# A hybrid decoder step: S5 of the prompt's second half moves beside the first two quarters' FFN

## The chip, the cores and the metric

The kernel runs on one core of one Trainium2 chip, in one launch. The metric is the device time of one execution in microseconds. The core has five engines that run their own instruction streams in order: TensorE (PE; PEld is its weight load), VectorE (DVE), ScalarE (ACT), GpSimd (POOL) and SyncE (SP), which here only issues DMA transfers. A wait of an instruction holds everything behind it on the same engine.

## The reference

One layer for a prompt of 2048 tokens and for 8 single-token samples; every weight product is in float32. What is computed, cut to what matters:

```python
n = rmsnorm(x, norm1_g)
proj = n @ w_in                      # 512 S5 inputs | 1536 qkv | 512 z | 4 beta | 4 a
y_s5  = s5_mixer(u_s5, ...)          # diagonal state space: complex scan over time, gelu, gate
y_gdn = gdn_mixer(qkv, z, beta, a)   # gated delta rule, 4 heads of 128, chunks; short conv; norm; gate
x = x + concat(y_s5, y_gdn) @ w_out
y = conv_ffn(rmsnorm(x, norm2_g))    # h = x @ w_up; conv of 3 taps over time; silu(gate)*up @ w_down
x = rmsnorm(x + y, normf_g)
```

Both mixers and the FFN's conv carry state along the prompt, so the quarters of the prompt are worked on in the order of time.

## The kernel before, in words

The prompt is cut in four quarters of 512 tokens, q0 to q3; the 8 samples ride behind q0. Activations stand transposed, channels on partitions. Every large product is made three times from splits of its operands in a high and a low part, `hi*hi`, `hi*lo`, `lo*hi` (`mm3`; `mm24` does it for the 8 channel tiles of the model, 24 matmuls for one tile of 128 outputs). Each 128x1024 piece of weights is loaded by SP into `wr` (2 buffers) and split into `whi` (a copy on ACT) and `wlo` (a subtraction on DVE); these come out of a ring of 8 buffers, `NW`.

The program has three stages.

- **Prologue.** For all four quarters in the order 3, 2, 1, 0: `x_load`, `norm_first` (transposes on PE, squares, row scales; x^T goes to DRAM) and `s5_in`, which multiplies with the S5 part of `w_in` and writes the inputs `up` to DRAM as `uD`. Beside them `s5_setup` computes the S5 matrices in eight steps, one per batch of 4 groups, and writes them to DRAM (`ED`, `FD`, `TD`). In that loop GpSimd's temporary `op`, the tile `Fi` and the tile `Tt` share one buffer, and so a step passes it on three times.
- **Mixers.** The string `MIXERS` is the order of emission: `b` and `h` are the two parts of one of eight S5 batches (`s5_batch`), each over all 256 chunks of 8 tokens; `F`, `I`, `B` are front, inverse and back of a delta net head. A batch loads its inputs `U` and matrices, multiplies, rotates, scans (one scan instruction per group and quarter, with `s5_turn` between quarters), rotates back and multiplies again, and ends with `s5_gelu`.
- **FFN.** The string `FFN` mixes `r`, the next piece of the generator `rest`, with the delta net stages of later quarters. `rest` first does the output gate of S5 (`s5_glu`) for q0 and q1, then for q2 and q3, then `ffn` for each quarter: the output projection in two halves of the tokens (`ffn_out`, the DVE addition L1144), norm 2 of the first half beside the second, a few tiles of the up projection early (`UPS`, first half of the tokens, which cover the second half's norm), and then eleven pieces of two channel tiles each (up projection, conv, gate, `ffn_down`). `N` makes the next quarter's normed input again from x^T in DRAM (`norm_again`).

The strings give the order of emission; a scheduler of the build then orders each engine's instructions from it, so the order on the engines is fixed before the kernel runs.

The normed input of a quarter lies in one buffer of the pool `n` (tag `nT`), so a new one waits for the last reader of the old one. PSUM tiles come in twos: `mm` for projections, `f` for many small things, `d` for the down projection, `s` for S5 (given back after the mixers).

Of the kernel before, what the change touches and what calls it, by code (L numbers as in the profile page):

```python
# [43 lines left out]
FFN = "IBNFrrIrFrrrrSrrBFrIIBrrrFIrBBrNFrIFrrrrBIrrFrrBIrrrrBFrrrrINBrFIrFrrBFIrrrrIrBrBrrrrrrrFrrrrrIBrrrGrrrrrrrrrrrrrrrrrrrr"  # L44
# columns of the constants
# [36 lines left out]
def rsqrt_(nc, a, y, t):  # L82
    """y = a^-1/2; one Newton step after exp/ln."""
# [9 lines left out]
def rsqrt_cols(c, ss, n, scale, tag, rows=128, tmp=None):  # L93
    """(ss*scale + eps)^-1/2 for ss [rows, n]"""
# [6 lines left out]
# ---------------------------------------------------------------- constants  # L101
def consts(c):
# [13 lines left out]
    # per-channel weights as columns  # L116
# [17 lines left out]
    # GDN  # L134
# [4 lines left out]
    # w_in columns for beta, a: [hi 8 | lo 8] per k tile  # L139
# [15 lines left out]
    # Xi[p, r, i] = (i == 4 (p % 8) + r): four rows of a 32 x 32 identity per partition  # L155
# [8 lines left out]
def sample_halos(c):  # L164
    """contribution of the samples' conv states to their conv outputs: [channel, sample]"""
# [69 lines left out]
    # row scales on all partitions  # L235
# [13 lines left out]
def norm_samples(c, pre):  # L249
    """normed x^T of the samples, [channel, (k tile, sample)]"""  # L250
# [41 lines left out]
def wsplit(c, src, eng=None):  # L292
    """[128, 1024] of weights as hi and lo"""
# [6 lines left out]
def wcols(c, w, col, q=None):  # L300
    """w[:, col:col+128] as hi and lo, [128, k, 128]"""
# [10 lines left out]
def proj(c, q, nT, w, col):  # L312
    """w[:, col:col+128]^T n, one PSUM tile per block of tokens"""
# [31 lines left out]
def s5_setup(c):  # L345
    """S5 matrices to DRAM: per batch of 4 groups T, F (input), E (output), tables."""
# [5 lines left out]
    c.ab1 = cp.tile([128, 2, 32], F32, name="ab1")   # re | signed im (-, +)  # L352
# [938 lines left out]
def kernel(tc, inp, outp):  # L1291
# [7 lines left out]
    with ExitStack() as es:  # L1299
# [154 lines left out]
```

## Time and profile before

| | |
|---|---|
| device time, median of 3 runs | 2872.86 us (2869.67 to 2876.55) |
| span of the profiled execution, first to last instruction | 2874.3 us |
| PE busy | 2715.0 us, 94% |
| weight loads busy | 2337.9 us, 81% |
| DVE busy | 2176.9 us, 76% |
| ACT busy | 1476.0 us, 51% |
| POOL busy | 609.6 us, 21% |

The profiled execution has no time of its own beside its span; the span lies within the three runs. A busy share is an average over the three stages, which differ; the ends of matmuls are modelled and neighbours overlap, so how fast PE works is read from the distance of starts.

### The profile page before, as it was taken

The page shows a single profiled execution, that of the slowest core. Times are in us where ns is not written, and L with a number is a line of the kernel's source. Part 1 is how long each engine was busy: PE and PEld are TensorE (multiplying, and loading weights), DVE is VectorE, ACT ScalarE, POOL GpSimd, SP SyncE. Part 2 cuts the span into 40 slices and gives each one's busy share as a digit, 9 for nine tenths or more (in the row PEclk, how much of TensorE's full clock was granted, in tenths as well). Part 3 has the DMA queues.
Part 4 walks back from the last instruction along what each step waited for, and adds up shares of the span by engine and source line. Part 5 has one row for each costly group of instructions (what it writes and reads, how often), then busy time and mean ns, then how long its engine had stood idle before and what let it go on. Part 6 is the DMA issues. An engine that isn't in the chain of part 4 may idle for free.

```text
span 2874.3 us, 45554 instructions
## 1 busy us (share of the span) xinstructions
PE 2715.0 (94%) x16103; PEld 2337.9 (81%) x16103; DVE 2176.9 (76%) x4964; ACT 1476.0 (51%) x3051; POOL 609.6 (21%) x970
## 2 busy tenths in 40 slices
PE   6998788899999999998899999999999998999998
PEld 4798676786888999998887888878888787888887
DVE  8949898856688787778588687887768667676666
ACT  4446565653665554455564554555545445444444
POOL 4325332100121122222221100113211112211112
PEclk9999887898999999999999999999999999999999
DMA  7644433453644232233533333245333334523332
GB/s 205 199 134 132 113 109 92 105 133 104 182 110 117 77 103 87 89 97 111 155 115 109 100 91 98 84 137 174 93 96 97 90 93 144 157 88 96 95 97 74
DMA packets 457657, 329.30 MB, mean 115 GB/s; under 512 B 74960, under 2 KB 412249, under 8 KB 457412
## 3 DMA queue, kind: packets, MB, share of 16 engines
q1 hardware_dynamic: 447091, 297.77, 35.8%
q0 software_dynamic: 10336, 28.61, 3.4%
q8 instruction: 127, 2.08, 0.3%
q14 instruction: 103, 0.84, 0.1%
HBM read 279.29 MB, written 47.29 MB: 114 GB/s over the span
## 4 chain that ended last, share of the span: by engine, by line
PE 66%; DVE 17%; DMA 8%; ACT 4%; issue 3%; POOL 0%; SPq 0%; DVEq 0%; POOLq 0%; ACTq 0%
PE psmm L287 15%; PE psmm L288 15%; PE psmm L289 15%; PE psd L287 5%; PE psd L288 5%; PE psd L289 5%; DVE wlo L72 3%; DVE t L823 1%; ACT whi L71 1%; DVE X L907 1%; DMA xr<-xTD 1%; DMA mr<-mixT 1%; DVE x L1097 1%; DVE hh L649 1%; DMA wr<-in_w_out_dram 1%
## 5 line engine op out<-in xcount | busy, mean ns | idle before, releaser
L287 PE MATMUL psmm<-nT,whi 128*128 128x512 f32 (+2 forms) x3232 | 1115.5, 347 | 45.2 <-ACT whi L71 9.6
L288 PE MATMUL psmm<-nT,whi 128*128 128x512 f32 (+2 forms) x3232 | 1110.3, 344 | 4.8 <-DVE nT L224 3.0
L289 PE MATMUL psmm<-nT,wlo 128*128 128x512 f32 (+2 forms) x3232 | 1107.2, 343 | 1.7 <-POOL wlo L72 1.0
L287 PEld LDWEIGHTS psmm<-nT,whi 128*128 128x128 f32 x3232 | 622.5, 193 | 120.3 <-ACT whi L71 11.7
L288 PEld LDWEIGHTS psmm<-nT,whi 128*128 128x128 f32 x3232 | 624.5, 193 | 73.1 <-DVE nT L224 4.5
L71 ACT ACTIVATE whi<-wr 128x1024 fp32r<-128x1024 f32 x404 | 427.2, 1059 | 496.3 <-PE psmm L288 309.9
L289 PEld LDWEIGHTS psmm<-nT,wlo 128*128 128x128 f32 x3232 | 623.0, 193 | 72.4 <-issue 1.9
L72 DVE TENSOR_TENSOR wlo<-wr,whi 128x1024 fp32r<-128x1024 f32 x388 | 482.3, 1246 | 193.2 <-ACT whi L71 187.4
L1097 DVE TENSOR_TENSOR x<-psd,x 128x512 f32<-128x512 f32 (+2 forms) x464 | 255.6, 558 | 127.3 <-PE psd L289 125.2
L287 PE MATMUL psd<-gt,whi 128*128 128x512 f32 (+2 forms) x928 | 323.6, 350 | 12.7 <-DVE x L1097 10.4
L288 PE MATMUL psd<-gt,whi 128*128 128x512 f32 (+2 forms) x928 | 316.5, 342 | 0.0
L289 PE MATMUL psd<-gt,wlo 128*128 128x512 f32 (+2 forms) x928 | 314.6, 340 | 0.0
L1254 DVE SCALAR_TENSOR_TENSOR t<-raw,cc,t 128x512 f32<-128x512 f32 x352 | 271.5, 772 | 37.1 <-ACT t L1251 27.5
L1255 POOL COPY halo<-raw 128x2 f32<-128x2 f32 x176 | 49.6, 282 | 850.7 <-DVE raw L1250 765.9
L1251 ACT ACTIVATE t<-raw,cc 128x512 f32<-128x512 f32 (+1 forms) x176 | 127.2, 723 | 170.0 <-DVE raw L1250 156.7
L287 PEld LDWEIGHTS psd<-gt,whi 128*128 128x128 f32 x928 | 175.0, 189 | 42.5 <-DVE x L1097 18.8
L72 POOL TENSOR_TENSOR gt<-s,gt 128x512 fp32r<-128x512 f32 (+1 forms) x88 | 134.7, 1531 | 350.4 <-ACT gt L71 341.6
L288 PEld LDWEIGHTS psd<-gt,whi 128*128 128x128 f32 x928 | 175.1, 189 | 20.6
L289 PEld LDWEIGHTS psd<-gt,wlo 128*128 128x128 f32 x928 | 174.9, 189 | 20.8
L1107 POOL TENSOR_TENSOR sq<-sq 128x256 f32<-128x256 f32 (+1 forms) x112 | 109.8, 981 | 219.1 <-ACT sq L1105 213.1
L906 DVE TENSOR_TENSOR tm<-X,N 128x124 f32<-128x124 f32 (+30 forms) x496 | 125.4, 253 | 26.7 <-DMA N<-nD 17.6
L907 DVE TENSOR_TENSOR X<-X,tm 128x124 f32<-128x124 f32 (+30 forms) x496 | 129.6, 261 | 8.4
(503 smaller groups left out, 3666.5 us busy)
## 6 DMA issues: line engine op xcount, KB each, us to landing
wr<-in_ffn_w_up_dram SPq DMA_DIRECT2D x176, 512.0 KB
wr<-in_ffn_w_down_dram SPq DMA_DIRECT2D x88, 512.0 KB
wr<-in_w_in_dram SPq DMA_DIRECT2D x64, 512.0 KB
wr<-in_w_out_dram SPq DMA_DIRECT2D x64, 512.0 KB
xTD<-xT SPq DMA_DIRECT2D x32, 256.0 KB
N<-nD SPq DMA_DIRECT2D x16, 512.0 KB
mr<-mixT SPq DMA_DIRECT2D x32, 256.0 KB
xr<-xTD SPq DMA_DIRECT2D x32, 256.0 KB
```

What stands on the lines that cost most here:

```text
L71: nc.scalar.activation(hi, raw, AF.Copy)
L72: (eng or nc.vector).tensor_tensor(lo, raw, f32(hi), op=OP.subtract)
L287: nc.tensor.matmul(out, lhsT=wh, rhs=xh, start=first, stop=False)
L288: nc.tensor.matmul(out, lhsT=wh, rhs=xl, start=False, stop=False)
L289: nc.tensor.matmul(out, lhsT=wl, rhs=xh, start=False, stop=last)
L906: nc.vector.tensor_tensor(m, X[:, :, j:j + 1].to_broadcast(sh), N[:, j:j + 1, j + 1:].to_broadcast(sh), op=OP.mult)
L907: nc.vector.tensor_tensor(X[:, :, j + 1:], X[:, :, j + 1:], m, op=OP.add)
L1097: nc.vector.tensor_tensor(x2[:, j, b0:b1], p, x2[:, j, b0:b1], op=OP.add)
L1107: c.nc.gpsimd.tensor_tensor(acc[0], acc[0], s, op=OP.add)
L1251: nc.scalar.activation(t[:, :n], raw[:, 2:2 + n], AF.Copy, scale=w[2])
L1254: nc.vector.scalar_tensor_tensor(t[:, :QT], raw[:, j:j + QT], w[j], t[:, :QT], op0=OP.mult, op1=OP.add)
L1255: nc.gpsimd.tensor_copy(c.halo[:, ch], raw[:, QT:QT + 2])
```

## The change

Prologue and mixers now handle only the first half of the prompt: `x_load`, `norm_first` and `s5_in` for q1 and q0, and eight S5 batches over 128 chunks (`HC`), which leave the state in `hst`. Two generators are new. `second` (letter `p` in the string) does load, norm and S5 inputs of q3 and q2 among the pieces of q0's FFN; it takes its four x tiles from the ring of weights and loads and splits the S5 part of `w_in` again for each of the two quarters. `third` (letter `t`) does the eight S5 batches of the second half, and then the gate of q2 and q3, among the pieces of q1's FFN; its matrices lie in the buffer `nT` (`s5_room`, two places), its PSUM tiles are `f`, and every batch loads its matrices from DRAM a second time. `norm_again` falls away for q2. The string `FFN` is new, and `UPS` has three tiles instead of four.

```diff
-NW, NWR, NV, NG, NM, UPB = 8, 2, 8, 4, 9, 1
+NW, NWR, NV, NG, NM, UPB = 8, 2, 8, 4, 10, 1
-UPS = (0, NCT, 1, NCT + 1)
+UPS = (0, NCT, 1)
-UNQ = (3, 2, 1)
+UNQ = (3, 1)
...
+FFN = ("IBNFrIrFSrBIrr"
+       "FrBIrFrBIrBrprprprprprprprprprprr"
+       "NFrIrFrBIrFrBIrFrtBIrtBrttrttrttrttrttrrr"
+       "NrFrIrFrBIrFrBIrFrBIrBrrrrGrrrr"
+       "rrrrrrrrrrrrrrrrr")
...
-def s5_batch(c, t, sp):
+def s5_batch(c, t, half, mk, samples):
...
-        nc.sync.dma_start(U[:, g], c.uD[t * 64 + g * 16:t * 64 + g * 16 + 16].rearrange("c s m -> s c m"))
+        nc.sync.dma_start(U[:, g], c.uD[t * 64 + g * 16:t * 64 + g * 16 + 16, :, m0:m0 + HC].rearrange("c s m -> s c m"))
...
-    for q in range(4):
+    if half:
+        nc.vector.tensor_copy(hh[:, :, 0, 0], c.hst[:, gs])
+    else:
+        nc.vector.memset(hh[:, :, 0, 0], 0.0)
+    for q in range(2):
...
             elif s == "N":
-                st.q, st.h, st.n = st.q + 1, 0, NT()
-                norm_again(c, st.q, st.n)
+                st.q, st.h = st.q + 1, 0
+                st.n = st.n2 if st.q == 2 else NT()
+                if st.q != 2:
+                    norm_again(c, st.q, st.n)
                 st.col = gdn_cols(c, st.q, st.n)
...
-            order = (3, 2, 1, 0)
-            xs = x_load(c, 3, pre)
+            xs = x_load(c, 1, pre)
...
-            for q0 in (0, 2):
-                yield from s5_glu(c, q0, nT)
+            yield from s5_glu(c, 0, nT)
...
+        def second():
+            xs = x_load(c, 3, None)
+            n = NT()
+            rs = norm_first(c, 3, n, xs)
+            yield
+            yield from s5_in(c, 3, n, None, None, rs)
+            xs = x_load(c, 2, None)
+            st.n2 = NT()
+            norm_first(c, 2, st.n2, xs)
+            yield
+            yield from s5_in(c, 2, st.n2, None, None, None)
+        def third():
+            maker = s5_room(c, np_)
+            bs = [s5_batch(c, t, 1, maker(t), False) for t in range(8)]
+            next(bs[0])
+            for t in range(8):
+                if t < 7:
+                    next(bs[t + 1])
+                next(bs[t], None)
+                yield
+            s5_final(c)
+            yield from s5_glu(c, 2, None, NT)
...
-            w, p = wcols(c, c.w_up, ch * 128), c.ps("mm" if len(ups) < 2 else "d")
+            w, p = wcols(c, c.w_up, ch * 128), c.ps("mm" if len(ups) < 1 else "d")
```

What that does to the order on the engines is seen at three places. On PE, the first S5 product of the mixers, ahead of the change; `Fm` and `U` are the matrix and the inputs of a batch, and the matmuls around it are the delta net's projections of q0.

```order
L287 MATMUL psmm<-nT,whi 128x264
L636 MATMUL pss<-U,Fm 128x256 x4
L288 MATMUL psmm<-nT,whi 128x264
L289 MATMUL psmm<-nT,wlo 128x264
L287 MATMUL psmm<-nT,whi 128x264
```

The same place on PE after the change:

```order
L289 MATMUL psmm<-nT,whi 128x256
L633 MATMUL pss<-U,Fm 128x128 x4
L290 MATMUL psmm<-nT,wlo 128x256
L288 MATMUL psmm<-nT,whi 128x256
L289 MATMUL psmm<-nT,whi 128x256
```

The product has half the columns. It stood 715 rows into PE's stream, and now stands 499 rows into it: the transposes and S5 inputs of two quarters are no longer ahead of it.

On DVE, q1's FFN, in a piece in the middle of the quarter, ahead of the change: `raw` and `t` are the conv of the up projection, `x_6015` takes the down projection's sums, and `De`, `LT`, `AT` belong to a delta net head.

```order
L1250 TENSOR_TENSOR raw<-psmm,rs_16639 128x256
L885 SCALAR_TENSOR_TENSOR LT<-psf,hc,De 128x128
L886 SCALAR_TENSOR_TENSOR AT<-psf,hc,De 128x128
L885 SCALAR_TENSOR_TENSOR LT<-psf,hc,De 128x128
L886 SCALAR_TENSOR_TENSOR AT<-psf,hc,De 128x128
L1254 SCALAR_TENSOR_TENSOR t<-raw,cc,t 128x512 x2
L1097 TENSOR_TENSOR x_6015<-psd,x_6015 128x512
```

Such a piece of q1's FFN on DVE after the change; `nT` is now the room of the S5 batch, `hw` the turn between quarters, `hst` the state that the next batch of the same groups starts from:

```order
L1129 TENSOR_TENSOR x_5295<-psd,x_5295 128x512
L639 TENSOR_TENSOR nT<-nT 128x8x64
L1296 TENSOR_TENSOR s<-s,t 128x512
L1129 TENSOR_TENSOR x_5295<-psd,x_5295 128x512
L649 SCALAR_TENSOR_TENSOR nT<-rho,nT 128x64 x4
L989 SCALAR_TENSOR_TENSOR rv<-psb,col,vt 128x128
L642 COPY nT<-hst 128x4
L601 TENSOR_TENSOR hw_17624<-nT 128x4
L601 TENSOR_TENSOR hw_17634<-nT 128x4
L586 SCALAR_TENSOR_TENSOR ga<-ga,psf 128x512
L600 TENSOR_TENSOR hw_17624<-hw_17624,nT 128x4
```

The scans, turns and gelu of an S5 batch stand between the additions of the down projection, in one in-order stream with them.

On DVE, the boundary from q0's FFN to q1's, ahead of the change: the additions of the output projection's second half (L1144), norm 2 (L195) and the splits of weights (L72).

```order
L1144 TENSOR_TENSOR x_6015<-psmm,xr 128x256
L833 TENSOR_TENSOR t<-s,t 128x512
L97 TENSOR_SCALAR rkq_a<-ssq,epscol 128x8
L195 SCALAR_TENSOR_TENSOR nrm<-x_6015,cc,rq 128x256
L72 TENSOR_TENSOR wlo<-wr,whi 128x1024
L1144 TENSOR_TENSOR x_6015<-psmm,xr 128x256
L195 SCALAR_TENSOR_TENSOR nrm<-x_6015,cc,rq 128x256
L72 TENSOR_TENSOR wlo<-wr,whi 128x1024
```

The same boundary on DVE after the change, where L1176 is that addition, L196 that norm and L938 and L939 the two instructions of a step of the delta net's inverse:

```order
L1176 TENSOR_TENSOR x_5295<-psmm,xr 128x256
L939 TENSOR_TENSOR X<-X,tm 128x4x25
L993 TENSOR_SCALAR vn<-psb,hc 128x128
L196 SCALAR_TENSOR_TENSOR nrm<-x_5295,cc,rq 128x256
L938 TENSOR_TENSOR tm<-X,N 128x4x24
L73 TENSOR_TENSOR wlo<-wr,whi 128x1024
L939 TENSOR_TENSOR X<-X,tm 128x4x24
L73 TENSOR_TENSOR nT_5296<-nrm,nT_5296 128x256
L1176 TENSOR_TENSOR x_5295<-psmm,xr 128x256
```

From the first addition of q1's output projection to the first `raw` of its up projection DVE had 118 rows, none of them of an inverse, and now has 311, of which 124 are the steps of two inverses.

## Rows read from the trace of the kernel before

**Rows 1.** The page: busy time of the engines over the span.

```profile
PE 2715.0 (94%) x16103; PEld 2337.9 (81%) x16103; DVE 2176.9 (76%) x4964; ACT 1476.0 (51%) x3051; POOL 609.6 (21%) x970
```

**Rows 2.** Busy time by stretches of the front: us, engines, granted PE clock, DMA.

```profile
0.00:749.00 749.00, 650.49 (x3851) 546.96 (x3852) 578.67 (x1762) 386.48 (x979) 197.59 (x242) 0.89 0.48 135
749.00:2874.30 2125.30, 2064.50 (x12254) 1790.96 (x12253) 1598.18 (x3202) 1089.52 (x2073) 412.00 (x728) 0.99 0.37 107
212.00:507.00 295.00, 245.41 (x1539) 212.42 (x1539) 258.78 (x734) 171.50 (x465) 103.26 (x116) 0.86 0.41 113
507.00:749.00 242.00, 226.90 (x1226) 181.94 (x1225) 164.61 (x495) 122.42 (x303) 22.99 (x37) 0.89 0.46 123
```

**Rows 3.** Busy time by stretches of the FFN stage, same columns.

```profile
839.00:1313.00 474.00, 470.87 (x3712) 449.39 (x3711) 374.16 (x886) 244.68 (x488) 108.03 (x211) 1.00 0.33 93
1471.00:1915.00 444.00, 441.10 (x2159) 354.08 (x2157) 356.53 (x772) 234.09 (x457) 58.41 (x125) 1.00 0.34 99
...
1312.70:1471.00 158.30, 141.82 (x1033) 130.29 (x1032) 112.19 (x253) 87.61 (x194) 37.43 (x49) 0.96 0.47 139
```

**Rows 4.** Timeline of PE in q1's FFN: start, us, instruction.

```profile
1839.68 0.39 PE L287 MATMUL psmm<-nT,whi 128*128 128x512 f32 x1
1839.91 0.39 PE L288 MATMUL psmm<-nT,whi 128*128 128x512 f32 x1
```

**Rows 5.** S5 inputs and first S5 product: count, durations, first to last start.

```profile
L550 DVE TENSOR_TENSOR up<-psmm,rsB x12: 1042/1090/1180, 42.4 to 146.9; 128x512 f32<-128x512 f32 x12
L548 ACT ACTIVATE up<-psmm x8: 366/384/385, 167.8 to 194.5; 128x256 f32<-128x256 f32 x8
...
L636 PE MATMUL pss<-U,Fm x64: 377/379/634, 212.2 to 463.5; 128*128 128x256 f32 x64
```

**Rows 6.** GpSimd's `op` in the setup, and waits between 26 and 170 us (total, times, longest).

```profile
L484 POOL TENSOR_TENSOR op<-CTim,PB x8: 1052/1063/1964, 63.0 to 160.4; 128x512 f32<-128x512 f32 x8
...
POOL op L484 <- DMA TD<-Tt: 37.4, 5, 9.4
```

**Rows 7.** GpSimd's timeline in the setup: its shortest link.

```profile
92.27 1.06 POOL L484 TENSOR_TENSOR op<-CTim,PB 128x512 f32<-128x512 f32 x1 [6.94 <-DMA TD<-Tt]
...
101.64 1.96 POOL L484 TENSOR_TENSOR op<-CTim,PB 128x512 f32<-128x512 f32 x1 [2.57 <-ACT nT L223]
```

**Rows 8.** DVE between 212 and 507 us: instructions on `hh`, then groups by line.

```profile
212.00:507.00 295.00, 22.28 (x64) 13.25 (x64) 87.20 (x223) 13.24 (x64) 18.11 (x8) 0.86 0.41 113
...
L593 DVE TENSOR_TENSOR yv<-pss,ga 128x512 f32<-128x512 f32 x14 | 9.5, 679 | 3.8 <-ACT ga L592 3.7
L589 DVE SCALAR_TENSOR_TENSOR ga<-ga,pss 128x512 f32<-128x512 f32 x14 | 9.5, 676 | 2.8 <-ACT ga L588 2.8
...
L603 DVE TENSOR_TENSOR hw<-hw,tab 128x4 f32<-128x4 f32 x32 | 6.1, 200 | 1.9 <-ACT hw L602 1.8
```

**Rows 9.** Timeline of PE: float32 products of S5, and smaller ones of a delta net head.

```profile
503.32 0.59 PE L668 MATMUL pss<-hw,Es 128*128 128x256 f32 x2
503.75 0.59 PE L665 MATMUL pss<-U,Tm 128*128 128x256 f32 x2
...
224.55 0.38 PE L954 MATMUL psb<-Sst,kq 128*128 128x128 f32 x2
224.78 0.39 PE L955 MATMUL psb<-Sst,kq 128*128 128x128 f32 x2
```

**Rows 10.** Groups by line: transposes of x, splits of weights, steps of the inverse.

```profile
L215 PE MATMUL psf<-ident,xt 128*128 128x128 f32 x128 | 23.6, 311 | 2.9 <-DVE nT L224 2.0 <-DVE nrm L195 0.7 <-DVE cc L132 0.2
...
L72 DVE TENSOR_TENSOR wlo<-wr,whi 128x1024 fp32r<-128x1024 f32 x388 | 482.3, 1246 | 193.2 <-ACT whi L71 187.4
L906 DVE TENSOR_TENSOR tm<-X,N 128x124 f32<-128x124 f32 (+30 forms) x496 | 125.4, 253 | 26.7 <-DMA N<-nD 17.6
L907 DVE TENSOR_TENSOR X<-X,tm 128x124 f32<-128x124 f32 (+30 forms) x496 | 129.6, 261 | 8.4
```

**Rows 11.** First and last addition of the output projection: durations, first to last start.

```profile
L1144 DVE TENSOR_TENSOR x<-psmm,xr x64: 405/423/433, 749.1 to 2490.4; 128x256 f32<-128x256 f32 x56, 128x264 f32<-128x264 f32 x8
```

More of the change, by code (lines that the diff above doesn't have):

```diff
@@ L199, in x_load @@
 def x_load(c, q, pre):
-    xs = [pre.tile([128, 1024], F32, name="xt", bufs=6) for _ in range(4)]
+    xs = [pre.tile([128, 1024], F32, name="xt", bufs=6) if pre else c.W("xt", F32) for _ in range(4)]
     for i, x in enumerate(xs):
-        (c.nc.sync if q == 3 else c.nc.gpsimd).dma_start(x, c.x_p[q * QT + i * 128:q * QT + (i + 1) * 128, :])
+        (c.nc.gpsimd if q == 0 else c.nc.sync).dma_start(x, c.x_p[q * QT + i * 128:q * QT + (i + 1) * 128, :])
     return xs
@@ L542, in s5_in @@
         rows = slice(t * 128, t * 128 + 128)
-        up = pre.tile([128, QT], F32, name="up", bufs=UPB).rearrange("p (s m) -> p s m", s=8)
-        for b0, b1, p in projw(c, q, nT, ws[t]):
+        up = (pre.tile([128, QT], F32, name="up", bufs=UPB) if pre else c.V("up")[:, :QT]).rearrange("p (s m) -> p s m", s=8)
+        for b0, b1, p in projw(c, q, nT, ws[t] if ws else wcols(c, c.w_in, t * 128)):
             e = min(b1, QT)
@@ L578, in s5_states, with s5_gelu @@
     c.ysm = sp.tile([16, 32, 8], F32, name="ysm")
-def s5_gelu(c, sp, out, y, rows=128):
+def s5_gelu(c, a, out, y):
     nc = c.nc
-    n = int(np.prod(y.shape[1:]))
-    a = sp.tile([128, 512], F32, name="ga", bufs=2)[:rows, :n]
-    if len(y.shape) == 3:
-        a = a.rearrange("p (a b) -> p a b", a=y.shape[1])
     nc.scalar.activation(a, y, AF.Square, scale=math.sqrt(0.044715))
@@ L613, in s5_batch @@
     lo, hi = slice(0, 64), slice(64, 128)
[L614 removed]
+    m0 = half * HC
+    U = mk("U").rearrange("p (g m) -> p g m", g=4)
     for g in range(4):
[L616 to L618 removed]
+        nc.sync.dma_start(U[:, g], c.uD[t * 64 + g * 16:t * 64 + g * 16 + 16, :, m0:m0 + HC].rearrange("c s m -> s c m"))
+    Fm, tab, Tm, Em, Es = (mk(n) for n in ("Fm", "tab", "Tm", "Em", "Es"))
     nc.sync.dma_start(Fm[:, :512], c.FD[t])
@@ L651, in s5_batch @@
     yield
[L653 to L654 removed]
+    s5_turn(c, hh[:, :, 1, 64], Ct, St, c.hst[:, gs])
+    hw = v65(mk("Xw"))[:, :, :, 0:64]
     H = hh[:, :, :, 0:64]
[L656 to L673 removed]
+    nc.gpsimd.tensor_tensor(hw, H, St[:, :, None, 0:64].to_broadcast(sh), op=OP.mult)
+    tt(H, H, Ct[:, :, None, 0:64].to_broadcast(sh), op=OP.mult)
+    yv = mk("yv")
+    p = c.ps(c.s5ps)
+    for g in range(4):
+        o = p[:, g * HC:(g + 1) * HC]
+        nc.tensor.matmul(o, lhsT=T[:, g], rhs=U[:, g], start=True, stop=False)
+        oq = o.rearrange("p (q m) -> p q m", q=2)
+        nc.tensor.matmul(oq, lhsT=E[:, g], rhs=H[:, g], start=False, stop=False)
+        nc.tensor.matmul(oq, lhsT=Es[:, g], rhs=hw[:, g], start=False, stop=True)
+    s5_gelu(c, mk("ga"), yv, p)
+    for g in range(4):
+        nc.gpsimd.dma_start(c.yD[t * 64 + g * 16:t * 64 + g * 16 + 16, :, m0:m0 + HC].rearrange("c j m -> j c m"), yv[:, g * HC:(g + 1) * HC])
+    if not samples:
+        return
+    p = c.ps(c.s5ps)
     for g in range(4):
@@ L683, in s5_batch, with s5_tiles, mk, s5_room @@
     nc.scalar.activation(c.ysm[:, gs], p[:16, 32:64].rearrange("p (g b) -> p g b", g=4), AF.Copy)
+def s5_tiles(c, sp):
+    kinds = dict(U=("U", 2), hh=("hh", 2), Xw=("Xw", 2), yv=("yv", 2), ga=("ga", 2))
+    def mk(n):
+        tag, bufs = kinds.get(n, ("mat", NM))
+        return sp.tile([128, 520], F32, name=n, tag=tag, bufs=bufs)[:, :520 if n in ("tab", "hh", "Xw") else 512]
+    return mk
+def s5_room(c, pool):
+    room = pool.tile([128, 16 * NQ], F32, name="nT")
+    sizes = dict(U=512, Fm=512, Tm=512, Em=512, Es=512, tab=520, hh=520, Xw=520)
+    state = {}
+    def maker(t):
+        def mk(n):
+            if n not in sizes:
+                return c.V(n)[:, :512]
+            at = (t % 2) * sum(sizes.values()) + sum(list(sizes.values())[:list(sizes).index(n)])
+            return room[:, at:at + sizes[n]]
+        return mk
+    return maker
 def s5_sample(c, sp):
@@ L1390 @@
         c.hst = c.cp.tile([128, 32], F32, name="hst")
+        c.s5ps = "s"
         with tc.tile_pool(name="s5", bufs=1, side="right") as sp:
             s5_states(c, sp)
-            bs = [s5_batch(c, t, sp) for t in range(8)]
+            mk = s5_tiles(c, sp)
+            bs = [s5_batch(c, t, 0, mk, True) for t in range(8)]
             hs = list(bs)
@@ L1404 @@
         ps_s.close()
+        c.s5ps = "f"
         c.wl = W2(nc)
@@ L1418, in rest @@
                 xrs, fin = yield from ffn(c, q, x2, nT, xrs, fin)
+        def second():
[20 more added lines that the diff above has]
+            yield from s5_glu(c, 2, None, NT)
         rs = rest()
+        se, th = second(), third()
         for s in FFN:
@@ L1422 @@
                 next(rs, None)
+            elif s == "p":
+                next(se, None)
+            elif s == "t":
+                next(th, None)
             else:
```

101 lines of the change are left out of this document (37 added, 64 removed).

## The prediction, made before the run

> **What bounds the kernel now.** I read the page's busy times first, then busy times by stretch, and last the timeline inside a stretch. The page gives PE 94% of the span and DVE 76% [rows 1], which suggests that PE is the bound throughout. The stretches say otherwise. Up to the first addition of the output projection, at 749.1 us [rows 11], PE is busy 650.5 of 749.0 us and DVE 578.7; behind it PE is busy 2064.5 of 2125.3 us [rows 2]. So nearly 100 of PE's 160 idle microseconds lie ahead of the FFN. In the middle of a quarter's FFN nothing is free on PE: 470.9 of 474.0 us and 441.1 of 444.0 [rows 3]. Since the ends of matmuls are modelled, I check this with starts: two 512-column matmuls of q1 stand 0.23 us apart and each is drawn 0.39 us long [rows 4], so the engine takes the next one in all the time. What is put into such a stretch lengthens it by its full work.
>
> The stage ahead of the FFN has three parts with different limits. (1) Until 212.2 us, when the first S5 product starts, the S5 inputs and the setup run; the last input's `up` starts at 194.5 us [rows 5]. The setup is a chain: GpSimd's `op`, `Fi` and `Tt` share a buffer, so a step's second `op` waits for the store of the last step's `Tt`; `op` starts from 63.0 to 160.4 us, seven steps of 13.9 us, and waits 37.4 us in that window for that store [rows 6]. (2) From 212 to 507 us DVE is busy 258.8 of 295.0 us, PE 245.4: the S5 batches and q0's delta net, where DVE is nearest to full [rows 2]. (3) From 507 to 749 us PE is busy 226.9 of 242.0 us [rows 2]: the output gate of four quarters, and projections.
>
> So the change takes work from a stage that is partly idle and puts it where PE has nothing to give. What it wins is idle time ahead of the FFN; what it costs is the moved matmuls at full price, and more DVE work at the boundaries between quarters.
>
> **The change part by part.** The sum goes against the profiled span of 2874.3 us, 1.4 over the median of 2872.86, which I take off at the end.
>
> (a) *Prologue.* The inputs of the first two of four quarters start at 42.4 us and the last at 194.5 us [rows 5]. That is about 40 us for a quarter, so the inputs of two are done near 115 us. Then the setup is last. With today's links it ends near 168 us (the last `op` at 160.4, then `Fi` and `Tt`), and a first product stands near 174: a saving of 38. Its shortest link, from 92.27 to 101.64 us, is 9.4 us [rows 7], where others wait for busy engines; eight such would end 31 us earlier, a saving of 69. Half of the work beside it is gone but the engines' queues still hold the delta net's first projections, so I take a value between, the first product at 162: **-50** (-38 to -69).
>
> (b) *S5 batches on half the columns.* DVE's instructions on `hh` take 87.2 us between 212 and 507, the three groups of gelu and turns 9.5, 9.5 and 6.1 [rows 8]: 112 us, of which half, 56, goes away. DVE is busy 259/295 there, so the stretch shortens by 56 x 295/259 = **-65**. If fixed costs of the smaller instructions keep a third of the saving, it is -46; if waits of GpSimd, ACT and transfers shrink along more than in proportion, -85.
>
> (c) *The gate of q2 and q3* leaves part (3): 192 matmuls of 512 columns at 0.232 us [rows 4] are 44.5 us, in a stretch that PE fills to 227/242: 44.5 x 242/227 = **-47**.
>
> (d) *What FFN gets on PE.* S5 inputs of two quarters: 2 x 4 tiles x 24 = 192 matmuls, 44.5 us. The gate, 44.5 us. S5's second half: 128 products of 128 columns; a float32 product of 256 columns starts every 0.43 us, and 128-column ones of a delta net head 0.23 us apart [rows 9], so 128 x 0.215 to 0.23 = 27.5 to 29.5, if they don't need the time of the large ones (55). Half of the 128 transposes of x, 23.6 us drawn [rows 10] with overlap: 8. Sum 125; I take **+124** (100 to 152).
>
> (e) *The rest on DVE, ACT and the queues.* The S5 part of `w_in` is split twice more: 8 subtractions of 1.246 us [rows 10] are 10 us on DVE, and as many copies on ACT; norm 1 of two quarters moves in, and the second making of q2's normed input falls away; SP gets the matrices of eight batches again and the weights, some 48 loads. In the middle of a quarter DVE is busy 374 of 474 and 357 of 444 us [rows 3], so this lies beside PE: **0**. Without that cover, where PE waits for a split, up to +15.
>
> (f) *DVE at the boundary from q0 to q1.* It took 158.3 us with PE busy 141.8 and DVE 112.2 [rows 3]. Between the output projection's additions and q1's up projection DVE now has the 124 steps of two inverses, which average 0.257 us [rows 10]: 32 us, and other rows of heads, which brings DVE's work there to some 171 us by the counts of rows and their durations, and PE's to about 139. A boundary that took PE plus 16 idle could take DVE's 171 plus some idle: about 180 us, **+20**. Below, 0, if the steps fall into the gaps between additions; above, +59, worked out among the rivals (R1).
>
> (g) *One tile less in `UPS`.* Norm 2 of a second half has 24 matmuls of 256 columns less to hide it. At half of 0.232 us each they are 2.8 us; for three boundaries, where PE also waits somewhat longer, **+5** (0 to +17). Behind those norms stand the splits of weights on DVE [rows 10], which are late next.
>
> Sum: -50 -65 -47 +124 +0 +20 +5 = -13; 2874.3 - 13 = 2861; with the median's 1.4 less it would be 2860, and since I rounded moved work down in (d), I write **2862**.
>
> *A rule against the reading of a full PE.* The trace shows q2's middle stretch with PE busy 441 of 444 us, and the weight loads 354 [rows 3]. The Trainium skill ("Perfetto Trace Analysis", section "Identifying the Most-Contended Engine") holds matmul busy time to be a bad measure, because matmuls are pipelined, and wants the weight loads' busy share instead. By the share of the loads a fifth of that stretch would be free, and (d) would cost 100 instead of 124. By the starts, 0.23 us apart without a gap [rows 4], it costs 124, which stands in the sum.
>
> **The rivals.**
>
> R1, *the boundary q0 to q1 becomes DVE's* (slower). The inverses are chains of small steps in one in-order stream with the additions that free PSUM for the output projection, so PE stops for each; a step also waits for the delta net's matmuls, which stand behind the output projection on PE. For it: DVE's work at the boundary exceeds PE's for the first time, by my count 171 against 139. Against it: the steps are 0.25 us each, and the inverse's waits in the trace are small against its work [rows 10]. Then DVE keeps its idle time of today's boundary, 158.3 - 112.2 = 46 us, beside 171 of work: 217 us, +59 and not +20, and the sum is 2862 + 39 = 2901. It decides from 12 us beyond (f) for no gain, some 17 for a measurable loss.
>
> R2, *nothing is won*: the smaller S5 instructions keep their fixed cost, (b) comes out at -46 or so and part (2) is set by q0's delta net instead. -50 -46 -47 +124 +20 +5 = +6, less the 1.4: 2879; with 5 more from (a), 2874. In (b), that DVE is full to 88% only speaks for it.
>
> R3, *weight loads are the bound* (faster). The moved matmuls cost 100: 2838. The starts in [rows 4] speak against it; for it, that PE stands only at 81% by loads [rows 1].
>
> R4, *the setup doesn't get shorter*, and the first S5 product is held to 174 us or later by the chain and by the tables behind it: (a) is -30, and the sum 2882. [...]
>
> **How the numbers follow.** What a measurement of this kernel can tell from no change is about 0.2%, 5.7 us: 2867.1 to 2878.6. Chances: the forecast 0.38 and R3 0.12, both faster; R2 0.12, the same; R1 0.28 and R4 0.10, slower. That makes faster 0.50, same 0.12, slower 0.38. The forecast's own range, from the bounds of (b), (d) and (f) that move against each other, is 2840 to 2867. The range for all goes down to 2800 (the lower bounds of (a) and (b) together, -39, with 2838) and up to 2925 (2901 with the upper bounds of (e) and (g), +27).
>
> **What would show it.** Right: the first S5 product near 162 us (143 to 174); the first addition of the output projection near 749 - 162 = 587 us; behind it some 2274 us instead of 2125, PE full in the middle of each quarter and the stretches of q0 and q1 longer by the moved work (65 and 75); the boundary q0 to q1 near 180 us. Wrong: a first addition later than 610 us puts the fault in (a) to (c); if the stage behind is longer than 2290 us, PE idle for additions at the boundary shows R1, and PE idle in the middle of q1 shows waits of the second half's S5 batches, whose scans and gelu stand between the additions of the down projection on DVE; I hold these covered, since the batches are begun one ahead, and this would make the prediction wrong in a place where no row of before can tell.

## The result, and the profile after

The changed kernel took 2989.77 us, the median of 4 runs (2984.88 to 2996.21), beside 2871.7 us for the kernel before in the same session: a ratio of 1.0404 (95% interval 1.0384 to 1.0424). It is 118 us slower, where a gain of 11 us was forecast, and lies beyond the range's upper end of 2925. The profiled execution has a span of 2994.4 us.

The page's row of busy times, after, answers to [rows 1].

```profile
PE 2764.4 (92%) x16287; PEld 2378.4 (79%) x16287; DVE 2176.9 (73%) x4984; ACT 1482.4 (50%) x3055; POOL 622.1 (21%) x1010
```

DVE does what it did before, to the tenth of a microsecond, and PE is drawn 49 us busier; nothing on this row explains 120 us. The marks of the prediction come next: the S5 products of either half, and the additions of the output projection (count; shortest, median and longest in ns; first to last start in us).

```profile
L633 PE MATMUL pss<-U,Fm x64: 270/275/377, 170.5 to 342.3; 128*128 128x128 f32 x64
L633 PE MATMUL psf<-nT x64: 270/275/377, 1537.4 to 1694.9; 128*128 128x128 f32 x64
...
L1176 DVE TENSOR_TENSOR x<-psmm,xr x64: 408/422/433, 643.6 to 2608.2; 128x256 f32<-128x256 f32 x56, 128x264 f32<-128x264 f32 x8
```

The first product stands at 170.5 us (forecast 162, from 143 to 174). The first addition stands at 643.6 us, where 587 was forecast and 749.1 was the time before [rows 11]. So the stage ahead of the FFN won 105.5 us and not 162, and the FFN stage took 2350.8 us and not 2274. Busy times by stretch, after (stretch; its length; busy time of PE, weight loads, DVE, ACT and POOL with their counts; granted PE clock; DMA share; GB/s):

```profile
0.00:170.50 170.50, 131.47 (x817) 116.56 (x818) 137.76 (x495) 62.71 (x142) 67.18 (x79) 0.87 0.56 160
170.50:363.60 193.10, 173.96 (x1340) 163.08 (x1339) 155.19 (x440) 112.21 (x309) 81.09 (x111) 0.88 0.47 127
363.60:643.60 280.00, 239.19 (x1236) 187.38 (x1236) 188.69 (x629) 127.36 (x344) 23.35 (x43) 0.79 0.37 100
...
750.20:1192.90 442.70, 428.09 (x3312) 413.28 (x3311) 288.91 (x517) 203.89 (x353) 97.52 (x193) 0.97 0.36 107
1192.90:1439.20 246.30, 207.98 (x1319) 179.56 (x1317) 171.66 (x430) 127.02 (x291) 41.94 (x61) 0.90 0.39 112
1439.20:1895.80 456.60, 454.37 (x2245) 372.34 (x2244) 357.43 (x742) 247.39 (x464) 98.54 (x163) 1.00 0.43 123
1895.80:2093.60 197.80, 164.34 (x1035) 142.54 (x1034) 138.53 (x313) 101.91 (x224) 36.06 (x51) 0.92 0.44 127
```

Four rows stand out against [rows 2, 3]. The S5 stretch (second row) is 102 us shorter, but the stretch behind it, up to the output projection (third row), is 38 us *longer*, with the lowest granted clock of all, 0.79, although half of the gate's matmuls left it. The boundary q0 to q1 (fifth row; from the last `raw` of one quarter to the first of the next) grew from 158.3 to 246.3 us and the boundary q1 to q2 (last row) from 111.4 to 197.8; in neither is DVE full, 70% in both. q1's pieces (sixth row) are full, as forecast. The boundary q1 to q2 before, in the same columns:

```profile
1914.90:2026.30 111.40, 104.14 (x794) 99.10 (x793) 86.20 (x183) 62.52 (x135) 34.26 (x39) 0.97 0.54 162
```

To see what is work and what is loss, I count each PE record at the distance between starts that its shape has when PE runs through: 0.230 us for 512 columns, 0.117 for 256, 0.216 and 0.111 for a float32 record of 256 and 128 (the lower quartile of all distances in both traces). A stretch's length less this sum, both in us, is called PE's lost time here: pauses, and matmuls that start further apart. It is an estimate; another price for the small records moves single rows by up to 4 us, in both kernels alike.

| stretch | time before, after | work before, after | lost before, after |
|---|---|---|---|
| to the first S5 product | 212.2, 170.5 | 157.6, 102.7 | 54.6, 67.8 |
| to the last S5 product (first half) | 294.8, 193.1 | 190.0, 133.9 | 104.8, 59.2 |
| to the first output projection | 242.1, 280.0 | 191.3, 176.8 | 50.8, 103.1 |
| q0's projection and norm | 89.8, 106.6 | 77.0, 85.9 | 12.8, 20.7 |
| q0's pieces | 473.8, 442.7 | 454.9, 409.2 | 18.9, 33.4 |
| boundary q0 to q1 | 158.2, 246.3 | 126.9, 181.1 | 31.4, 65.2 |
| q1's pieces | 443.9, 456.6 | 427.6, 443.6 | 16.3, 13.0 |
| boundary q1 to q2 | 111.5, 197.8 | 95.8, 146.7 | 15.6, 51.1 |
| q2's pieces | 366.0, 418.3 | 360.8, 403.2 | 5.3, 15.1 |
| the rest | 482.0, 482.5 | 440.1, 439.5 | 41.9, 43.1 |
| sum | 2874.3, 2994.4 | 2522.0, 2522.7 | 352.3, 471.7 |

The work is the same, as it must be where the same products are only moved. All of the 120 us is lost time: 20 us more ahead of the FFN, where less was to be lost, and 99 more in it, 69 of them at two boundaries. The lengths hold one more thing: the boundaries hold 54 and 51 us more of PE's work, mostly of heads that stood in the pieces before. What such a loss looks like, on PE's timeline at the boundary q1 to q2, after (start, us, instruction, and the idle time before it with its releaser):

```profile
1933.16 0.66 PE L1228 MATMUL psd<-ident,x 128*128 128x128 f32 x4 [0.26 <-ACT yout L1230]
1942.70 0.61 PE L799 MATMUL psmm<-nT,wab 128*16 128x512 f32 x1 [8.89 <-ACT nT L72]
1943.11 0.41 PE L288 MATMUL psmm<-nT,whi 128*128 128x256 f32 x1
1943.32 0.42 PE L289 MATMUL psmm<-nT,whi 128*128 128x256 f32 x1
```

PE meets, in its order, the first product of the delta net's columns, whose input `norm_again` (letter `N`) is still to make, and pauses for 8.9 us. Behind the pause the 256-column matmuls of the output projection start 0.21 us apart instead of 0.117: the granted clock is at the lower of its two levels, 1.2 GHz. So the pause costs more than its length. PE's largest waits at the two boundaries (total us, times, longest), q0 to q1 first:

```profile
PE psmm L288 <- DVE x L1176: 6.7, 1, 6.7
PE psf L805 <- ACT abT L801: 6.7, 1, 6.7
...
PE psmm L288 <- DVE x L1176: 8.9, 3, 8.0
PE psmm L799 <- ACT nT L72: 8.9, 1, 8.9
```

Followed back on the other engines, three of these four longest waits (6.7, 6.7, 8.0 and 8.9 us) end in a transfer from or to DRAM that an engine meets in its order. Behind the 8.9 us for `nT` stands the load of x^T for `norm_again`. Behind the 6.7 us for the addition stands the load of an inverse's matrix (the tile `N`, not the letter): DVE waits for it, does 12 instructions of the inverse, and only then comes to the addition that PE waits for. Behind the 6.7 us for `abT` ACT waits 6.8 us for the store of a state. The lines of the addition's wait and of the load of x^T, in the order of time:

```profile
1296.66 0.88 DVE L938 TENSOR_TENSOR tm<-X,N 128x124 f32<-128x124 f32 x1 [6.09 <-DMA N<-nD]
1301.38 0.42 DVE L1176 TENSOR_TENSOR x<-psmm,xr 128x256 f32<-128x256 f32 x1
1301.86 0.58 PE L288 MATMUL psmm<-nT,whi 128*128 128x256 f32 x1 [6.74 <-DVE x L1176]
...
1941.23 0.75 DVE L196 SCALAR_TENSOR_TENSOR nrm<-xT,cc,rsB 128x512 f32<-128x512 f32 x1 [8.43 <-DMA xT<-xTD]
```

These four are 30 of the 72 us that PE pauses at the two boundaries; the rest is many short pauses.

What is there at the boundaries that was not? Counted by their lines, 2 fronts and 2 inverses of heads in the first (before: 1 and 0.1), 2 fronts and 1 inverse in the second (before: none of either). The new `FFN` string puts `N` and the next quarter's heads there, since the S5 work takes the buffer `nT` in the middle of the quarter.

### The profile page after: what moved, and what is told of

Its sections match the earlier page's. It is cut to its first block, busy times and chain, and to the rows that moved or that the text cites. A ratio compares the mean times of both kernels' runs of the same rounds, so it can differ in the third digit from the quotient of the medians.

```text
span 2994.4 us, 46166 instructions
## 1 busy us (share of the span) xinstructions
PE 2764.4 (92%) x16287; PEld 2378.4 (79%) x16287; DVE 2176.9 (73%) x4984; ACT 1482.4 (50%) x3055; POOL 622.1 (21%) x1010
## 5 line engine op out<-in xcount | busy, mean ns | idle before, releaser
L288 PE MATMUL psmm<-nT,whi 128*128 128x512 f32 (+2 forms) x3208 | 1114.5, 348 | 50.5 <-DVE x L1176 22.4
L288 PEld LDWEIGHTS psmm<-nT,whi 128*128 128x128 f32 x3208 | 622.0, 194 | 127.6 <-ACT t L852 15.6
L72 ACT ACTIVATE whi<-wr 128x1024 fp32r<-128x1024 f32 x412 | 435.1, 1059 | 549.5 <-PE psmm L289 358.7
L938 DVE TENSOR_TENSOR tm<-X,N 128x124 f32<-128x124 f32 (+30 forms) x496 | 119.5, 241 | 37.9 <-DMA N<-nD 24.6
L939 DVE TENSOR_TENSOR X<-X,tm 128x124 f32<-128x124 f32 (+30 forms) x496 | 126.1, 254 | 8.9
```

What stands on the lines that cost most here:

```text
L288: nc.tensor.matmul(out, lhsT=wh, rhs=xh, start=first, stop=False)
L938: nc.vector.tensor_tensor(m, X[:, :, j:j + 1].to_broadcast(sh), N[:, j:j + 1, j + 1:].to_broadcast(sh), op=OP.mult)
L939: nc.vector.tensor_tensor(X[:, :, j + 1:], X[:, :, j + 1:], m, op=OP.add)
```

## The experiments

Two theories stood at the start. T1: PE loses time where a head's chain stands beside too few independent matmuls, at the boundaries above all. T2: the moved S5 work itself costs more than its matmuls. Medians are set beside the kernel before in the same session, 2870.9 to 2873.5 us; ratios are to it, with their 95% interval.

**The heads spread.** In all strings below, only what differs from the changed kernel is shown, from q0's pieces to the end of q3's heads.

```diff
-prprprprprprprprprprrNFrIrFrBIrFrBIrFrtBIrtBrttrttrttrttrttrrrNrFrIrFrBIrFrBIrFrBIrB
+prpprpprpprpprpNrFrIFrBIrFrBIrrrrrrFBIrBrttrttrttrttrttrttrNFrIFrBIrrrrrrFrBIrFrBIrB
```

> The changed kernel with another order string only: the delta net heads of q2 and q3, which stood at the boundaries q0 to q1 and q1 to q2, begin in the last pieces of the quarter ahead, and the S5 batches of the second half run later in q1. Same work. Theory T1 (PE loses time where a head's chain stands beside too few independent matmuls, so at the boundaries): the two boundaries, 246 and 198 us, come back to about 180 and 115, some 15 to 30 us of it are given back in the pieces that take the heads, and the time falls by 50 to 120 us, to 2870 to 2940. Rival T2 (the moved S5 work itself costs more than its matmuls, by waits in the pieces where it stands): the time stays within 15 us of 2990.

2950.54 us (ratio 1.0268, 1.0242 to 1.0293): 39 us back. The two boundaries in its profile:

```profile
1287.00:1418.50 131.50, 111.31 (x863) 104.59 (x862) 97.65 (x243) 62.74 (x126) 36.90 (x43) 0.95 0.45 135
1943.10:2062.40 119.30, 106.06 (x821) 98.99 (x820) 95.41 (x233) 61.93 (x129) 29.89 (x39) 0.96 0.51 153
```

Lost time is 34 and 25 us there, against 65 and 51; q1's pieces lose 30 instead of 13. T2 falls as the cause of the boundaries: the S5 work stood in the same quarters. Of the 118 us, 77 remain.

**Three tiles in `UPS`, in the kernel before.**

```diff
-UPS = (0, NCT, 1, NCT + 1)
+UPS = (0, NCT, 1)
```

> The kernel before with three tiles in UPS instead of four, the first in the mm buffers and two in the d buffers, as after the change. T1 and T2 alike: three boundaries lose the cover of 24 matmuls of 256 columns, 2.8 us each or somewhat more: 2872 to 2890. If it were the cause of the slow boundaries, it would be 2950 and more.

2878.78 us (1.0018, 1.0003 to 1.0034): 5 us, which is term (g).

**The same with the heads at the boundaries.** S5, norm and gate of the kernel before, `UPS` of three, and its string from q0's projection on as the changed kernel's without its `p` and `t`. (With four tiles in `UPS` this order deadlocks, so the run above is its measure.)

```diff
-FFN = "IBNFrrIrFrrrrSrrBFrIIBrrrFIrBBrNFrIFrrrrBIrrFrrBIrrrrBFrrrrINBrFIrFrrBFIrrrrIrBrBrrrrrrrFrrrrrIBrrrGrrrrrrrrrrrrrrrrrrrr"
+FFN = "IBNFrrIrFrrrSrrBIrFrBIrFrBIrBrrrrrrrrrrrrNFrIrFrBIrFrBIrFrBIrBrrrrrrrrNrFrIrFrBIrFrBIrFrBIrBrrrrGrrrrrrrrrrrrrrrrrrr"
```

> The kernel before with three tiles in UPS (which alone measured 2878.8) and with the heads of q2 and q3 at the boundaries in the changed kernel's order; S5, norm and gate stand as before the change. T1 (a head's chain beside too few independent matmuls loses PE's time): after one string changed the boundaries q0 to q1 and q1 to q2 are 40 to 90 us longer, part of it the heads' own matmuls, and the time is 2915 to 2970. T2 (the moved S5 work costs more than its matmuls): 2865 to 2890.

2955.49 us (1.0284, 1.0266 to 1.0302): 77 us more than with `UPS` alone. The boundaries are nearly those of the changed kernel, 246.30 and 197.80 us there:

```profile
1222.30:1482.50 260.20, 208.30 (x1322) 178.54 (x1321) 181.93 (x448) 132.39 (x299) 43.94 (x61) 0.90 0.40 116
1861.60:2057.00 195.40, 164.35 (x1035) 142.72 (x1034) 138.54 (x313) 102.03 (x224) 38.11 (x51) 0.92 0.45 128
```

The order of the heads alone makes them, without any S5 work moved. The run also parts the 118 us: 5 for `UPS`, 77 for the order, and the 34 us from here to the changed kernel for the move itself. By lost time, the move costs 25 us in q0's pieces (8 here, 33 in the changed kernel, with the same heads there) and about 17 ahead of the FFN.

**Norm and S5 inputs into the gate's stretch, all heads spread.** Besides the string, `second` keeps row scales for q2 as it does for q3, and `norm_again` runs for q2 as well.

```diff
-IBNFrIrFSrBIrrFrBIrFrBIrBrprprprprprprprprprprrNFrIrFrBIrFrBIrFrtBIrtBrttrttrttrttrttrrrNrF...
+IpBprSrpprpprpprpprrrNrFrIrFrBIrFrBIrFrBIrtBrttrttrttrrrrrrttrttrtNrFrIFrBIrFrBIrFrBIrBrrrrrrNrF...
```

> The changed kernel with norm and S5 inputs of q3 and q2 in the stretch of the output gate, the heads of q1, q2 and q3 spread over the middles of q0, q1 and q2, the second half's S5 batches at the end of q0's FFN and the start of q1's, and q2's normed input made a second time. T1: the gate's stretch, where PE lost 103 of 280 us, takes the 52 us of moved matmuls with less than 20 us of added time, the boundaries come back as in the run with spread heads, and the time is 2830 to 2890. T2: 2930 or more, as with spread heads alone.

2999.86 us (1.0448, 1.0423 to 1.0472): a miss. The first output projection comes at 592.8 us, 51 earlier, but with two fronts fewer ahead of it; the pieces of q1 and q2, with four heads each, lose 43 and 28 us (13 and 15 in the changed kernel), the boundary q1 to q2 still 51. T1 as I had it was too simple: heads cost lost time in the middles too when they stand one behind the other.

**The gate with one product of three.** Only q0 and q1.

```diff
-mm3(nc, p[:, :b1 - b0], h4[:, kt, s], l4[:, kt, s], yT[:, K, 0, b0:b1], yT[:, K, 1, b0:b1], kt == 0, kt == 3)
+nc.tensor.matmul(p[:, :b1 - b0], lhsT=h4[:, kt, s], rhs=yT[:, K, 0, b0:b1], start=kt == 0, stop=kt == 3)
```

> The changed kernel with one of the three products in the output gate of q0 and q1, so 128 matmuls of 0.23 us, 29.7 us, are left out. T1, for the stretch from the last S5 product of the first half to the first addition of the output projection: it is set by the delta net's chains, not by PE's work, so it shortens by less than 12 us, and the whole by no more. Rival T3: PE's work sets it, and it shortens by 25 to 35 us.

2964.54 us (1.0326, 1.0304 to 1.0348): 25 us of the 29.7 come back, 21 of them in this stretch (280.0 to 258.6). That is less than T3's 25 to 35 and well over T1's 12, so T3 is nearer and T1 is wrong for this stretch. Its row:

```profile
358.10:616.70 258.60, 213.05 (x1038) 162.23 (x1037) 187.19 (x625) 125.38 (x343) 22.58 (x43) 0.74 0.40 108
```

PE's pauses and the gate's matmuls stand mostly one behind the other, not side by side: 112 us are still lost, and the granted clock falls to 0.74. So the gate's matmuls do cost most of their time there, as term (c) says.

**Half of S5, in the kernel before: term (b) alone.** The edit is cut to two of its places.

```diff
-    for q in range(4):
+    for q in range(2):
...
-            nc.tensor.matmul(p[:, g * NCH:(g + 1) * NCH], lhsT=F[:, g0 + g], rhs=U[:, g0 + g], start=True, stop=True)
+            nc.tensor.matmul(p[:, g * NCH:g * NCH + 128], lhsT=F[:, g0 + g], rhs=U[:, g0 + g, :128], start=True, stop=True)
```

> The kernel before with S5 on the first 128 of the 256 chunks only; the outputs of the second half are copies of the first half's (each written twice), so half of S5's matmuls, scans and gelu are left out and nothing is put elsewhere. This is the prediction's term (b) by itself. The prediction (VectorE sets the S5 stretch): 46 to 85 us less, 2788 to 2827. Rival (the time follows PE's work, and what PE loses there stays): 27.5 us of matmuls, at the lower clock of that stretch up to 40, so 2833 to 2848.

2870.69 us: a ratio of 0.999 (0.9972 to 1.0008). Half of S5 is worth nothing measurable (-8 to +2 us). Its first addition of the output projection, and the two stretches ahead of it:

```profile
L1145 DVE TENSOR_TENSOR x<-psmm,xr x64: 407/424/433, 739.4 to 2485.1; 128x256 f32<-128x256 f32 x56, 128x264 f32<-128x264 f32 x8
...
211.80:434.30 222.50, 184.76 (x1330) 171.78 (x1329) 168.03 (x495) 120.39 (x357) 95.43 (x135) 0.83 0.43 120
434.30:739.40 305.10, 273.23 (x1445) 215.24 (x1444) 203.48 (x624) 150.05 (x388) 28.38 (x49) 0.87 0.42 112
```

S5 ends 73 us earlier, and the stretch behind it takes 63 us more: the same picture as in the changed kernel. Both my forecast and its rival were off.

**Nearly no inverse, in the kernel before, then with half of S5.** The second has the edit above too.

```diff
-    for j in range(31):
+    for j in range(1):
```

> The kernel before with 30 of the 31 steps of each delta net inverse left out; PE's work stays. Halving S5 there gave nothing, so the stretch from the first S5 product to the output projection must be set by something else. If it is the chain of the delta net's heads, of which the inverse is the longest link on VectorE (62 steps of 0.25 us): the first addition of the output projection comes 25 to 60 us earlier, nearly all of it in that stretch, and the FFN stage changes by less than 12 us: 2810 to 2850. If it is the transfers or GpSimd: 2862 or more.

> The kernel before with both cuts at once: S5 on 128 chunks with the second half's outputs copied, and 30 of 31 steps of each inverse left out. Alone they brought the first addition of the output projection 9.7 and 22.4 us earlier in their profiles. If the two chains bound the stage side by side, each covering the other's saving, both together bring it 50 us or more earlier, and the time is 2825 or less. If they only add (32 us), 2835 to 2850; if something else bounds the stage below, 2850 or more.

2852.86 us (0.994, 0.9923 to 0.9958) and 2824.68 us (0.9825, 0.9799 to 0.9852). The first additions, of the one and of the other:

```profile
L1144 DVE TENSOR_TENSOR x<-psmm,xr x64: 406/424/433, 726.7 to 2476.9; 128x256 f32<-128x256 f32 x56, 128x264 f32<-128x264 f32 x8
```

```profile
L1145 DVE TENSOR_TENSOR x<-psmm,xr x64: 406/424/434, 690.7 to 2436.7; 128x256 f32<-128x256 f32 x56, 128x264 f32<-128x264 f32 x8
```

Against 749.1 us, half of S5 brings it 9.7 us forward, the inverses 22.4, both together 58.4; in the medians it is nothing, 18 and 49 us. (The inverses alone stay just short of their expectation, 25 us and 2850.) More than the sum comes back, so two chains, S5's and the heads', share the stage, and each covers what the other gives up.

**Nearly no inverse, in the changed kernel** (the same edit).

> The changed kernel with 30 of the 31 steps of each delta net inverse left out, 960 of VectorE's instructions, about 235 us of its time; PE's work stays. T1 (the chains of the heads make PE wait and run at the low clock where little else is at hand): PE's lost time falls where heads stand outside the middles, in the gate's stretch and at the boundaries q0 to q1 and q1 to q2, by 40 to 110 us in all, in the middles by less than 15. T4 (the backs' and fronts' own links, not the inverse, hold PE up): less than 20 us in all.

2942.69 us (1.0247, 1.0221 to 1.0272): 47 us less, but in the wrong place for T1: the two stretches ahead of the output projection lose 38 us less (124 instead of 162), the two boundaries only 7. The steps of the inverse are not what the boundaries lose. What leads into them was left: the first step still waits 6.1 us for `N` from DRAM, then DVE 1.7 and 1.5 us for two more transfers, and PE's wait for the addition at q0 to q1 is still 6.7 us.

**`N` two pieces earlier, heads as they are.**

```diff
-prprrNFrIrFr ... ttrttrrrNrF
+prpprNrrFrIrF ... ttrttrNrrrF
```

> The changed kernel with one letter moved in two places: N (the next quarter's normed input and the delta net's columns) stands two pieces earlier, in the last pieces of q0's and q1's FFN, while the heads stay at the boundaries. If the waits for N's normed input and columns, which PE meets in order at the boundary (6.7 and 8.9 us the longest, with the low granted clock behind them), are most of what the boundaries lose, the two lose 25 to 50 us less and the time is 2940 to 2965. If the heads themselves are: less than 12 us, 2978 or more.

2971.18 us (1.0343, 1.0323 to 1.0363), between the two expectations: the boundary q1 to q2 shrinks from 197.8 to 163.3 us and loses 26 instead of 51, with the wait of 8.9 us gone; q1's pieces give 8 us of it back; the boundary q0 to q1 stays as it was.

```profile
1194.10:1437.20 243.10, 204.85 (x1304) 179.19 (x1303) 170.88 (x426) 125.98 (x282) 45.07 (x61) 0.90 0.39 113
1909.00:2072.30 163.30, 148.55 (x977) 132.12 (x976) 125.29 (x285) 94.31 (x205) 37.45 (x51) 0.96 0.49 140
```

**The heads of q2 out of the boundary q0 to q1, `N` as it is.**

```diff
-NFrIrFrBIrFrBIrFrtBIrtBrttrttrttrttrttrrrN
+NrrrrrFrIFrBIFrBIFrtBIrttBrttrttrttrttrtrN
```

> The changed kernel with the heads of q2 moved from the boundary q0 to q1 into q1's pieces, N left where it stands, and q2 to q3 unchanged. If the heads make that boundary slow, its 246 us come to 150 or less, with the heads' two fronts (56 us of matmuls) going to q1's pieces, and the time is 2950 to 2975. If N or the rest of the boundary does: the boundary keeps 20 us or more of its 34 us of added loss, and the time is 2980 or more.

2976.71 us (1.0365, 1.0348 to 1.0381), 2 us over the expected range. The boundary halves, and loses 30 instead of 65 us; q1's pieces, with four heads and S5, lose 37 instead of 13. So 24 of the 35 us move along with the heads.

```profile
1185.60:1309.50 123.90, 104.55 (x778) 96.85 (x778) 82.15 (x159) 58.89 (x111) 35.58 (x43) 0.93 0.48 144
1309.50:1868.80 559.30, 547.93 (x2750) 445.94 (x2749) 443.87 (x1014) 309.08 (x636) 102.36 (x181) 0.98 0.41 116
```

So at q0 to q1 it is the heads; at q1 to q2, 25 of the 51 us go with `N`.

**The setup's `Tt` in another buffer**, in the changed kernel, and then in the kernel before.

```diff
-            To = sp.tile([128, 4, 8, 16], F32, name="Tt", tag="op")
+            To = sp.tile([128, 4, 8, 16], F32, name="Tt", tag="ot")
```

> The changed kernel with the setup's Tt in the buffer of VectorE's temporary ot instead of GpSimd's op, so that GpSimd's next op no longer waits for the store of Tt. If that chain sets the first S5 product (170.5 us), the product comes 15 to 40 us earlier and the time falls by 5 to 35 us; if VectorE or the queues set it, both stay within 6 us.

> The kernel before with the setup's Tt in the buffer of VectorE's ot. In the changed kernel this one line gave 11 us, although the first S5 product came 36 us later. If the gain comes from an order on PE that starts q0's projections ahead of that product, it may come here too: 2855 to 2873. If the setup's chain matters only after the change, since it is the last thing in the prologue only there: within 6 us of 2872.

2978.7 us (1.0371, 1.035 to 1.0393) and 2896.33 us (1.0083, 1.006 to 1.0106). The first S5 product comes later in the changed kernel, not earlier:

```profile
L633 PE MATMUL pss<-U,Fm x64: 270/275/580, 206.2 to 352.3; 128*128 128x128 f32 x64
```

The edit only changes the store that GpSimd waits for: `op` now waits 27.8 us for that of `Fi`, where it waited 33.6 for that of `Tt`. The order changed too: 29 us more of PE's work stand ahead of the first S5 product. So the run leaves open whether GpSimd's chain sets 170.5 us. What the start of S5 is worth stays open too: in the changed kernel the first product comes 36 us later and the time is 11 us less; in the kernel before it comes 12 us later (224.4), the first addition 25 us later (774.1), and the time is 25 us more, which neither expectation had.

**The best of these together**: heads spread, three S5 inputs to a piece, `Tt` in `ot`.

```diff
-prprprprprprprprprprrNFrIrFrBIrFrBIrFrtBIrtBrttrttrttrttrttrrrNrFrIrFrBIrFrBIrFrBIrB
+prppprppprppprNrFrIrFrBIrFrBIrrrrrrFrBIrBrttrttrttrttrttrttrNFrIrrrrrrFrBIrFrBIrFrBIrB
```

> The changed kernel with the heads of q2 and q3 spread over the ends of q0's and q1's FFN as in the first run, but begun a piece earlier or later so that no stage stands between q0's last piece and q1's first one, with norm and S5 inputs of the second half three to a piece, and with Tt in VectorE's buffer. T1: the boundaries as in the first run, 10 to 20 us less from Tt: 2915 to 2945; it doesn't reach the kernel before, as the middles give back some of it. If spreading could win all that the change lost, it would be 2870 or less.

2932.64 us (1.0217, 1.019 to 1.0243). It loses 416 us in all, the kernel before 352: 13 more ahead of the FFN, 12 in q0's projection, 21 in q0's pieces, the rest in q1 and q2. None of these versions beats the kernel before.

## Why the prediction was wrong, step by step

- **(d) was right in size, and the reading of the FFN stage in part.** (d) said +124; the work of the FFN stage, counted at full pace, rose from 1983.1 to 2109.3 us, +126. That is a count of matmuls and no test of R3. What speaks against R3's 100 is how times went with work: +52 us for 42 of work in q2's pieces, +13 for 16 in q1's, and in the whole stage +226 for 126. The Trainium skill ("Perfetto Trace Analysis", section "Identifying the Most-Contended Engine") names the weight loads' busy share, beside the share of peak, in place of matmul busy time. In q1's pieces the trace does not agree: the loads are busy 372 of 457 us, and PE has no room. But the pieces of q0 and q1 did not grow by 65 and 75: q0's went from 473.8 to 442.7 and q1's from 443.9 to 456.6, since the new string takes heads out of them. The prediction had not followed where the heads go.
- **(a) was about right**: -41.7 us against -50, inside its bounds, though no run shows that the setup's chain, from which it was worked out, sets the time. **(g)** was right: +5 forecast, and measured alone in the kernel before.
- **(b) failed.** The step was "the stretch shortens by 56 x 295/259 = -65", from DVE's busy 259 of 295 us (the product is 64). Taken out alone, half of S5 gave 9.7 us of the stage in the profile and nothing measurable in the time. The stretch was not DVE's: two chains share it, S5's and that of the heads, and the heads' chain fills the room that S5 leaves, as the three runs without half of S5, the inverses and both show. (b) and (c) together were to give 112 us and gave 63.8. Rival R2 named the heads, but priced (b) at -46 still; its bounds, -46 to -85, came from shares of DVE's work and left out the case that the stretch is not DVE's.
- **(c) was nearly right**: 29.7 us of gate matmuls left out gave 25, so the 44.5 are worth some 38 (44.5 x 25/29.7), against 47; this is an estimate, carried over from the other half's gate in the changed kernel. The 9.7 and the 38 make 48 of the 63.8 that (b) and (c) gave together; no run says where the other 16 come from.
- **(f) failed, and is the largest miss.** It priced one boundary at +20, with DVE's 171 us of work against PE's 139 as what counts. DVE's 171.7 us are as counted, but in 246 us; PE's work there is 181 at full pace, since a second front came along. The boundary q0 to q1 lost 34 us more, and the boundary q1 to q2, which wasn't priced at all, 35 more. R1 has the direction, at 217 us for the boundary, and one wait of 6.7 us has its form: additions behind an inverse in DVE's stream. But R1 has DVE as the bound, idle for 46 us; it is idle for 75, and ahead of that addition it waits for a load. PE's pauses in the order of its own stream, for heads and for `N`, and the low clock behind them make the loss; the order alone cost 77 us.
- **(e) was 0, and this failed too**: q0's pieces lose 14.5 us more than before, near the bound of +15, but 25 more than with the same heads and no moved work, 8 us, in the run with `UPS` of three. There q2's pieces and q0's projection lose as much as in the changed kernel, 10 and 8 us more than before, so that part is the order of the heads.

In sum: forecast -50 -112 +124 +25, measured -41.7 -63.8 +126.2 +99.4, in profiles. The first three were to win 38 us; measured, they lose 21. So even without the boundaries the move would not have paid: with the heads in the same order on both sides it costs 34 us. Small slips in the sums change nothing: two thirds of 65 is 43, not 46, and 2901 + 27 is 2928, not 2925.

Open is which links make the boundary q0 to q1 lose its time beyond the two waits followed above (the inverse's steps are 7 us at both boundaries together), and what sets the first S5 product at 170.5 us. No run took the loads and stores at the boundaries away, so what they cost in all is read from waits and not shown. A second `nT` buffer, which might let the heads run a quarter ahead beside the S5 work, was not tried.

## What to carry to other kernels

Moving work from a stage with idle time into a full one wins only as much lost time as it removes; count a stage's work at full pace and its loss apart, and ask which chain causes the loss and whether it is the one that you make shorter. A busy share of 0.88 on an engine did not make the stage that engine's here: two chains interleaved on it, each covered the other's saving, and only taking out both showed it. When a buffer's new use forces other stages together, price the place where they land, at every repetition of it, and follow the longest waits there back to their ends: here three of four ended in a DRAM transfer that an in-order engine met.

## What the runs showed of the hardware

A pause of PE was dearer than its length. Behind 8.9 us of waiting, 256-column matmuls started 0.21 us apart instead of 0.117, at the 1.2 GHz level of the granted clock. In the stretch from 363.6 to 643.6 us, the granted clock averaged 0.79, and the matmuls there were drawn busy for 239 us of what is 177 at full pace. Of the 103 us lost in it, 41 are pauses. The other 62 are matmuls drawn longer than that pace, most of them at the low clock: a mean of 0.79 between 1 and a half puts some 118 us at the lower level, an estimate.
